# A hybrid decoder step on one core: the sample convolution gathered, tied ranks counted, masks fused, and the down projection built from 2x2 block products

## The chip, the cores and the metric

One core of one Trainium2 chip. The metric is the device time of one execution of the whole program in microseconds (us). Before the change it is 1780.9 us, the median of 3 runs (1780.2 to 1784.61).

## What is computed

One layer of a decoder serves a prompt of 1024 tokens and 8 sample sequences of one token each, with the same weights (model width 1024, all float32):

```
q, k, v, idx, gdn = split(rmsnorm(x) @ w_in)
o_attn = attention over the 256 best keys, chosen by the indexer's score
         (lax.top_k: among equal scores the lower position wins)
cq, ck, cv = silu(causal conv of width 4 over gdn's q, k, v)   # sample tokens: 3 stored columns + 1 new
o_gdn  = gated delta rule(cq, ck, cv)
x += concat(o_attn, o_gdn) @ w_out
x += cross attention into 256 memory tokens
x += (silu(rmsnorm(x) @ w_gate) * (rmsnorm(x) @ w_up)) @ w_down     # D_FF = 2816 = 22 * 128
```

A prompt token chooses 256 keys out of up to 1024, a sample token 256 out of 4097.

## The kernel before

Activations lie transposed, 128 features on the partitions and the 1032 tokens along the columns. A float32 product is made of three matmuls: weights and activations are each split into a high part (a cast on ScalarE, line 125 for weights, 143 for activations) and a low part (the difference, GpSimd in line 126 for weights, VectorE in line 144 for activations), and high x high, high x low and low x high are summed in PSUM. `load_w` fetches a weight tile on SyncE's queue (SP) and splits it; `wh` and `wl` have two buffers each.

The program is written as generators that take turns (`run`), with the two top-k searches as side threads. The Tile framework then orders the instructions of each engine by priority and by its own timeline; each engine runs its list in that order, each wait in its place.

**The front** (0 to about 518 us) projects all columns of w_in. `gdn_front` makes the convolution for each of 12 column tiles; in a tile's last group it also convolves the 8 sample tokens, with four VectorE operations of 8 columns (lines 734 to 737). `stage_topk` searches the 256th best score of each prompt row bit by bit and writes a mask (lines 397 to 423). `stage_sample_topk` does the same for the sample tokens in seven-way steps: `count` compares 257 columns with up to seven thresholds, one VectorE operation each (line 1267), sums across partitions by a matmul and takes a digit. It runs the search three times: over the high 16 bits, over the low 16 bits, and (`radix(y, 13)`, line 1313) over the positions of the scores that are equal to the last one taken, 1 + 4 x 7 counts in five rounds. Its last operation is line 1314. Then the pools of the front are released, and attention begins with `stack_k` (lines 497 to 500) and `stack_q` (line 509) in their place.

**Attention and the memory part** run to about 1190 us and aren't touched but for names of scratch tensors.

**The gated units** (`unit_product`, to about 1512 us): gate and up projections of 2 x 128 features in each of 11 units, by products of 2x2 blocks (Strassen's form in Winograd's version, 7 products for 8). A unit leaves three of its four result blocks (the first is made earlier, in `early`); GpSimd multiplies them (line 1900) and SP stores them to `scrF`, features by tokens.

**The down projection** (`stage_down`, `down`) is plain. It goes through the 22 feature tiles in three passes (8, 7 and 7), each over 8 output tiles; a pass loads a weight tile of 8 or 7 x 128 x 128, multiplies it in three column groups (512, 256, 264) and adds each bank to the residual `xT` (line 1913). `fetch` brings activations back from `scrF` and splits them. The last pass ends each output tile with `store_y`: nine transposes on TensorE, copies, and DMAs.

```
self.down(0, acts, (0,))        # 8 feature tiles, first 512 columns
self.down(0, acts, (1, 2))
self.down(8, more, (0, 1, 2))   # 7
self.down(15, acts[:7], (0, 1, 2), True)
```

Of the kernel before, what the change touches and what calls it, by code (L numbers as in the profile page):

```python
# [6 lines left out]
F32 = mybir.dt.float32  # L7
# [32 lines left out]
class Kernel:  # L40
# [112 lines left out]
    def consts(self):  # L153
        nc, c = self.nc, self.c
        jp = c.tile([128, 128], I32, name="jp")
# [175 lines left out]
    def stage_topk(self):  # L331
# [62 lines left out]
        for j, i in enumerate(tl):  # L394
            nk = (i + 1) * 128
            eq = self.tk.tile([128, 1024], BF, name="tkeq", tag="eq")
            V.tensor_scalar(eq[:, :nk], hi[i], H[:, j:j + 1], None, op0=OP.is_equal)
            w = self.tk.tile([128, 1024], U16, name="tkw", tag="w")
            V.tensor_scalar(w[:, :nk], lo[i], sg[:, j:j + 1], ag[:, j:j + 1], op0=OP.mult, op1=OP.add)
            V.tensor_mul(lo[i], w[:, :nk], eq[:, :nk])  # L400
            yield
# [4 lines left out]
        for j, i in enumerate(tl):  # L406
# [4 lines left out]
            x = self.tk.tile([128, 1024], BF, name="tkx", tag="x")[:, :nk]  # L411
            pj, hj = P[:, j:j + 1], H[:, j:j + 1]
            V.tensor_scalar(eq, hi[i], hj, None, op0=OP.is_equal)
            V.tensor_scalar(x, lo[i], pj, None, op0=OP.is_equal)
            V.tensor_mul(eq, eq, x)
# [3 lines left out]
            V.tensor_scalar(x, lo[i], pj, None, op0=OP.is_gt)  # L419
            V.tensor_add(m, m, x)  # L420
            V.tensor_scalar(x, hi[i], hj, None, op0=OP.is_gt)
            V.tensor_add(m, m, x)
# [281 lines left out]
    def gdn_front(self, h):  # L704
# [3 lines left out]
        for kind, col, ct in (("k", C_GK, 4 + h), ("q", C_GQ, h), ("v", C_GV, 8 + h), ("z", C_GZ, None)):  # L708
            wh, wl = self.load_w(w_in[:, col + 128 * h:col + 128 * h + 128], KD, 128)
            j = "kqvz".index(kind)  # L710
            for g, (g0, n) in enumerate(GROUPS):
# [7 lines left out]
                else:  # L719
# [11 lines left out]
                    if g == 2:  # L731
                        st = self.stT[:, ct].rearrange("p (b j) -> p j b", j=3)
                        ys, us = y[:, m:n], raw[:, 4 + m:4 + n]
                        V.tensor_scalar(ys, st[:, 0], w[0], None, op0=OP.mult)
                        V.scalar_tensor_tensor(ys, st[:, 1], w[1], ys, op0=OP.mult, op1=OP.add)
                        V.scalar_tensor_tensor(ys, st[:, 2], w[2], ys, op0=OP.mult, op1=OP.add)
                        V.scalar_tensor_tensor(ys, us, w[3], ys, op0=OP.mult, op1=OP.add)
                        nc.gpsimd.tensor_copy(self.ctail[:, :, ct], raw[:, 1 + m:4 + m])
                        nc.gpsimd.tensor_copy(self.cnew[:, :, ct], us)
                    self.silu(y[:, :n], y[:, :n])  # L740
                nc.scalar.dma_start(self.scrG[h, j, :, g0:g0 + m], y[:, :m])
                if g == 2:
                    nc.gpsimd.tensor_copy(self.gsam[:, h, j], y[:, m:n])
                yield

# [428 lines left out]
    def sample_consts(self):  # L1174
# [49 lines left out]
        y = iota("i_pos", [128, 8, 32], [[-2, 8], [-128, 32]], 8191, 0)  # L1224
# [4 lines left out]
        V.tensor_scalar(off[:, 0:1], u, -16.0, None, op0=OP.mult)  # L1229
        V.tensor_scalar(u, pr, 3, 1, op0=OP.logical_shift_right, op1=OP.bitwise_and)  # L1230
        V.tensor_sub(off[:, 0:1], off[:, 0:1], u)
        self.rpos = I([128, 260], F32, name="rpos")
        V.memset(self.rpos, 8191.0 - 4096.0)
        V.tensor_scalar(self.rpos[:, 0:256], y.rearrange("p a b -> p (a b)"), off[:, 0:1], None, op0=OP.add)
# [10 lines left out]
    def stage_sample_topk(self):  # L1245
# [12 lines left out]
        y = kp.tile([128, 260], U16, name="sk_y")  # L1258
# [542 lines left out]
    def first(self, u, kind, s1, p, sg):  # L1801
# [5 lines left out]
        else:  # L1807
            V.tensor_add(sg[:, 1], s1, p)  # L1808
            self.nc.gpsimd.tensor_mul(sg[:, 1], sg[:, 0], sg[:, 1])
            self.nc.sync.dma_start(self.scrF[2 * u, :, 0:HN], sg[:, 1])  # L1810

    def unit_product(self, u):
# [9 lines left out]
        for kind in ("gate", "up"):  # L1822
# [69 lines left out]
            c = [u1, u2[:, :HN], s1]  # L1892
            if kind == "gate":
                for x in c:
                    self.silu(x, x)
                sg["c"] = c
            else:
                f = 2 * u
                for x, y, dst in zip(c, sg["c"], (self.scrF[f, :, HN:], self.scrF[f + 1, :, 0:HN], self.scrF[f + 1, :, HN:])):
                    nc.gpsimd.tensor_mul(x, x, y)  # L1900
                    nc.sync.dma_start(dst, x)

    def down(self, f0, acts, groups, last=False):
        nc, V = self.nc, self.nc.vector
        kt = len(acts)
        for o in range(KD):
            wh, wl = self.load_w(self.i["w_down"][0][128 * f0:128 * (f0 + kt), 128 * o:128 * o + 128], kt, 128)
            for g in groups:
                g0, n = self.G[g]
                p = self.bank("g", "pd")  # L1910
                self.proj(wh, wl, 0, 128, g, p, kt=kt, act=lambda k: [x[:, g0:g0 + n] for x in acts[k]])
                x = self.xT[:, o, g0:g0 + n]
                V.tensor_add(x, x, p[:, :n])  # L1913
            if last:
                self.store_y(o)

    def store_y(self, o):
        nc = self.nc
        cs = slice(128 * o, 128 * o + 128)
        for half in range(2):  # L1920
            p = self.bank("g", "py")
            for t in range(4):
                c = 128 * (4 * half + t)
                self.tr(p[:, 128 * t:128 * t + 128], self.xT[:, o, c:c + 128], 128)
            y = self.unit("y", [128, 4, 128])
            (nc.vector.tensor_copy if half else nc.scalar.copy)(y, p.rearrange("p (t c) -> p t c", c=128))
            nc.sync.dma_start(self.o["y_prompt"][0, 512 * half:512 * half + 512, cs].rearrange("(t p) c -> p t c", p=128), y)
        p = self.bank("g", "py")
        self.tr(p[:NS, :128], self.xT[:, o, T:NT], 128)
        y = self.unit("y8", [NS, 128])  # L1930
        nc.scalar.copy(y, p[:NS, :128])
        nc.scalar.dma_start(self.o["y_sample"].rearrange("b o d -> (b o) d")[:, cs], y)

    def fetch(self, f, h, l, s):

        a = self.unit("af")[:, :s.stop - s.start]
        self.nc.sync.dma_start(a, self.scrF[f, :, s])
        self.split(a, h[:, s], l[:, s])

    def stage_down(self, after_units):  # L1940

        acts = [(self.AH[:, k], self.AL[:, k]) for k in range(KD)]
        n1, n2, n = slice(0, HN), slice(HN, NT), slice(0, NT)
        for f in range(8):
            self.fetch(f, *acts[f], n1)
        after_units()
        for o in range(KD):
            self.nc.sync.dma_start(self.xT[:, o, n1], self.scrT[:, o, n1])  # L1948
        for f in range(8):
            self.fetch(f, *acts[f], n2)  # L1950
        self.down(0, acts, (0,))
        for o in range(KD):
            self.nc.sync.dma_start(self.xT[:, o, n2], self.scrT[:, o, n2])
        self.down(0, acts, (1, 2))
        more = [[self.du.tile([128, UW], FR, name="d" + x, tag="d")[:, :NT] for x in "hl"] for _ in range(7)]
        for f in range(8, 15):
# [140 lines left out]
```

## Time and profile before

| | |
|---|---|
| median of 3 runs | 1780.9 us |
| the profiled execution | 1789.59 us, of which its span 1787.4 us |
| busy: PE, PEld, DVE, ACT, POOL | 91%, 81%, 62%, 49%, 46% of the span |
| matmuls | 11316 |
| granted TensorE clock, mean | 0.952 of full speed |
| DMA | 206.44 MB, mean 115 GB/s |

The profile is of one execution, 8.7 us above the median. PE is TensorE's matmuls, PEld its weight loads, which run beside them; DVE is VectorE, ACT ScalarE, POOL GpSimd. A share of the whole span is a mean over stages with different limits, so the stages are looked at one by one. Matmuls are pipelined: the duration of one is longer than its distance to the next, and it is the distance that counts.

### The profile page before, as it was taken

To read this page: it belongs to the slowest core of one execution; us is meant where nothing else is said; L and a number is where in the kernel's file an instruction comes from. 1 tells how busy PE (TensorE), PEld (TensorE's weight loads), DVE (VectorE), ACT (ScalarE), POOL (GpSimd) and SP (SyncE) were. 2 spreads that over 40 slices of the span, in tenths; PEclk is the share of its full clock that TensorE was granted. 3 is DMA by queue.
4 is the path that set the end of the run, shared out by engine and by line. 5 is a ranking of instruction groups with operands and counts; after the bars stand their busy time and mean duration, and the time that the engine had idled before them with its cause. 6 is when DMAs were issued, how large, how long until landed. Compare 5 with 4: busy or idle time off the path is not lost. (4 is left out here: it accounts for less than half of the span.)

```text
span 1787.4 us, 31531 instructions
## 1 busy us (share of the span) xinstructions
PE 1634.5 (91%) x11316; PEld 1442.3 (81%) x11316; DVE 1106.3 (62%) x2913; ACT 880.8 (49%) x2069; POOL 827.7 (46%) x791
## 2 busy tenths in 40 slices
PE   6999988768859999989998899879999999899998
PEld 5989877768747777768896578669999999599998
DVE  7699996999979777762355523775556666313111
ACT  5568879964546666664565564432222323212111
POOL 1277663573147133225553436765656566342210
PEclk9999998879979899979998999989999999999999
DMA  4134354324242324256322244553444444922132
GB/s 156 46 91 130 118 145 125 119 90 134 85 121 63 82 72 122 78 156 184 89 83 59 79 140 148 190 160 101 137 125 126 130 131 132 313 82 86 42 90 58
DMA packets 268630, 206.44 MB, mean 115 GB/s; under 512 B 31397, under 2 KB 240506, under 8 KB 268338
## 3 DMA queue, kind: packets, MB, share of 16 engines
q1 hardware_dynamic: 249674, 175.34, 32.6%
q0 software_dynamic: 4864, 14.69, 2.9%
q10 hardware_dynamic: 13936, 14.40, 2.3%
q8 instruction: 89, 1.46, 0.3%
q14 instruction: 67, 0.55, 0.1%
HBM read 152.01 MB, written 52.47 MB: 114 GB/s over the span
## 5 line engine op out<-in xcount | busy, mean ns | idle before, releaser
L126 POOL TENSOR_TENSOR wl<-raw,wh 128x1024 fp32r<-128x1024 f32 (+2 forms) x107 | 255.3, 2387 | 401.8 <-ACT wh L125 329.0
L48 PE MATMUL pm<-AH,wh 128*128 128x384 f32 (+7 forms) x792 | 269.8, 341 | 4.6 <-ACT y L111 4.0
L48 PE MATMUL pm<-AH,wl 128*128 128x384 f32 (+7 forms) x792 | 263.0, 332 | 0.1
L48 PE MATMUL pm<-AL,wh 128*128 128x384 f32 (+7 forms) x792 | 262.7, 332 | 0.1
L125 ACT CAST wh<-raw 128x1024 fp32r<-128x1024 f32 (+2 forms) x107 | 110.0, 1029 | 255.5 <-PE pd L48 172.4
L48 PEld LDWEIGHTS pm<-AH,wh 128*128 128x128 f32 (+1 forms) x792 | 154.0, 195 | 12.0 <-ACT y L111 4.6
L1842 POOL TENSOR_TENSOR sl<-S,sh 128x512 fp32r<-128x512 f32 x88 | 119.7, 1371 | 89.6 <-ACT sh L1841 86.9
L48 PEld LDWEIGHTS pm<-AL,wh 128*128 128x128 f32 (+1 forms) x792 | 154.0, 194 | 6.7 <-issue 0.8
L48 PEld LDWEIGHTS pm<-AH,wl 128*128 128x128 f32 (+1 forms) x792 | 152.9, 193 | 5.1 <-issue 0.7
L1913 DVE TENSOR_TENSOR xT<-xT,pd 128x256 f32<-128x256 f32 (+2 forms) x72 | 36.8, 512 | 190.5 <-PE pd L48 190.4
L1841 ACT CAST sh<-S 128x512 fp32r<-128x512 f32 x88 | 53.3, 619 | 183.5 <-DVE S L1836 170.6
L48 PE MATMUL pd<-AH,wh 128*128 128x512 f32 (+2 forms) x360 | 116.3, 325 | 5.1 <-ACT wh L125 5.1
L48 PE MATMUL pd<-AH,wl 128*128 128x512 f32 (+2 forms) x360 | 115.4, 322 | 3.7 <-POOL wl L126 3.7
L48 PE MATMUL pd<-AL,wh 128*128 128x512 f32 (+2 forms) x360 | 115.1, 321 | 0.0
L1836 DVE TENSOR_TENSOR S<-raw 128x512 f32<-128x512 f32 x44 | 54.8, 1246 | 92.0 <-DMA raw<-in_w_gate 38.0
L48 PE MATMUL p<-AL,sh 128*128 128x260 f32 x352 | 99.7, 283 | 0.0
L48 PE MATMUL p<-AH,sh 128*128 128x260 f32 x352 | 99.6, 283 | 0.0
L48 PE MATMUL p<-AH,sl 128*128 128x260 f32 x352 | 99.3, 283 | 0.0
L48 PE MATMUL pg<-AH,wh 128*128 128x512 f32 x176 | 73.3, 419 | 14.6 <-DVE sg L1808 7.5
L1866 DVE TENSOR_TENSOR uu<-uu,p 128x260 f32<-128x260 f32 x176 | 71.9, 420 | 16.4 <-PE p L48 14.7
L48 PEld LDWEIGHTS pd<-AH,wh 128*128 128x128 f32 x360 | 68.1, 189 | 11.9 <-ACT wh L125 6.8
L48 PEld LDWEIGHTS pd<-AH,wl 128*128 128x128 f32 x360 | 67.9, 189 | 10.6 <-POOL wl L126 5.3
(703 smaller groups left out, 5153.8 us busy)
## 6 DMA issues: line engine op xcount, KB each, us to landing
raw<-in_w_gate SPq DMA_DIRECT2D x33, 512.0 KB
raw<-in_w_up SPq DMA_DIRECT2D x33, 512.0 KB
raw<-in_w_in SPq DMA_DIRECT2D x24, 512.0 KB
raw<-in_w_out SPq DMA_DIRECT2D x16, 512.0 KB
raw<-in_w_down SPq DMA_DIRECT2D x16, 512.0 KB
af<-scrF SPq DMA_DIRECT2D x14, 516.0 KB
raw<-in_w_down SPq DMA_DIRECT2D x16, 448.0 KB
scrG<-y ACTq DMA_DIRECT2D x32, 192.0 KB
```

Source lines behind the costliest of these rows:

```text
L48: return self.nc.tensor.matmul(out, lhsT, rhs, start=start, stop=stop)
L125: self.nc.scalar.copy(wh, raw)
L126: self.nc.gpsimd.tensor_sub(wl, raw, f32(wh))
L1836: op(t, x, y)
L1841: nc.scalar.copy(h, x)
L1842: nc.gpsimd.tensor_sub(l, x, f32(h))
L1866: V.tensor_add(out[:, c], x[:, c], p[:, :w // 2])
L1913: V.tensor_add(x, x, p[:, :n])
```

## The change

Four edits. (1) The 48 small operations of the sample convolution become seven over all 12 tiles at once, and three SiLUs. (2) Ties of the sample top-k are ranked by a running sum along the columns and seven small matmuls across partitions, in place of the third search. (3) In the prompt's masks a comparison and the product or sum after it become one instruction. (4) The down projection is made of seven products of 2x2 blocks. The units now store seven operands of 11 x 128 features to `scrD` (one of 512 columns from `early`, one more of 512, five of 520), with one more subtraction on GpSimd and three operations on VectorE for each unit; the weights' sums are made on VectorE while the stage runs, in two half steps of 6 and 5 feature tiles for each of four output tiles; `fetches` bring the next product's operands while one is computed.

```
 gdn_front, last group of a tile:
-  V.tensor_scalar(ys, st[:, 0], w[0], None, op0=OP.mult)
-  V.scalar_tensor_tensor(ys, st[:, 1], w[1], ys, ...)
-  V.scalar_tensor_tensor(ys, st[:, 2], w[2], ys, ...)
-  V.scalar_tensor_tensor(ys, us, w[3], ys, ...)
+def conv_sample(self):            # once, before the last z tile
+  for t in range(4):
+    V.tensor_tensor(z if t else y, x[t], w, op=OP.mult)      # 128 x 12 x 8
+    if t:
+      V.tensor_add(y, y, z)
+  for j, c in enumerate((4, 0, 8)):
+    self.silu(self.gsam[:, :, j], y[:, c:c + 4])
 stage_topk, each of six tiles (three such pairs more, and one ahead of the second search):
-  V.tensor_scalar(x, w, need[:, j:j + 1], None, op0=OP.is_le)
-  V.tensor_mul(m, x, eq)
+  V.scalar_tensor_tensor(m, w, need[:, j:j + 1], eq, op0=OP.is_le, op1=OP.mult)
 stage_sample_topk:
-  V.tensor_mul(y[:, :N], eq[:, :N], self.rpos[:, :N])
-  yield from radix(y, 13)
-  V.scalar_tensor_tensor(sel[:, :N], y[:, :N], P, sel[:, :N], op0=OP.is_ge, op1=OP.add)
+  V.memset(run[:, 0:1], 0.0)
+  V.tensor_copy(ep.rearrange("p (g j) -> p j g", j=8), eq[:, :256]...)
+  V.tensor_tensor_scan(run[:, 1:], ones, ep, 0.0, op0=OP.mult, op1=OP.add)
+  ...                                        # 4 bf16 matmuls of 256 columns, 3 of 1
+  V.scalar_tensor_tensor(w[:, :256], p[:, :256], need, eq[:, :256], op0=OP.is_le, op1=OP.mult)
+  V.scalar_tensor_tensor(w[:, 256:257], ...)
+  V.tensor_add(sel[:, :N], sel[:, :N], w[:, :N])
+def down_blocks(self, u, b11, up, gate):      # end of each unit; store() is a DMA on SP
+  G.tensor_mul(b12, b12, t3); G.tensor_mul(b22, b22, t2); G.tensor_mul(b21, b21, t4)
+  store(5, b22); store(6, b21)
+  V.tensor_sub(t3, b22, b12); store(3, t3)
+  V.tensor_sub(b12, b12, b11); store(1, b12)
+  G.tensor_sub(t2, b22, b12); store(2, t2)
+  V.tensor_sub(t4, b21, t2); V.tensor_scalar(t4[:, HN:], t2[:, HN:], -1.0, ...); store(4, t4)
 stage_down:
+order = ((0, HN, "A11"), (4, w, "A22"), (1, w, "S1"), (2, w, "S2"), (5, w, "S4"), (3, w, "S3"), (6, HN, "A12"))   # w = 520
+def weights(name, m, ks):                     # S: SBUF, get(i, j): DMA of a block into one of 3 buffers
+  A11, A12: split of the block;  A22: DMA into t = S[:, m, ks]
+  S1: V.tensor_add(t, t, get(2, 1))    S2: V.tensor_sub(t, t, get(1, 1))
+  S4: V.tensor_sub(t, get(1, 2), t)    S3: V.tensor_sub(t, get(1, 1), get(2, 1))
+  return self.split_w(t)
+def finish(name, m, banks):                   # banks added to x (residual) or U, on VectorE
+  A11: ACT copy; S1: two adds a bank; A22, S2, S3: one G.tensor_add more; S3: one V.tensor_add more
+for q, (_, n, name) in enumerate(order):
+  for m in range(4):
+    for ks in (slice(0, 6), slice(6, 11)):
+      wh, wl = weights(name, m, ks)
+      for p, c in zip(banks, halves):         # 1 x 512 or 2 x 260 columns
+        for k in range(ks.start, ks.stop):
+          self.three(p, wh[k], wl[k], h[:, c], l[:, c], ...)
+      one residual DMA, two fetches of the next product
+      store()                                 # output halves that are done
+    done += finish(name, m, banks)
 build: du has 6 buffers (was 14), on the side of the released pools; xT, U, S and wd beside it
```

## Rows read from the trace of the kernel before

**Rows 1.** the page's span in 40 slices of 44.7 us, busy tenths
```profile
PE   6999988768859999989998899879999999899998
...
DVE  7699996999979777762355523775556666313111
```

**Rows 2.** view of stages: busy us of each engine (instructions), then PEclk, DMA share, GB/s
```profile
330.00:465.00 135.00, 101.17 (x579) 93.34 (x578) 130.83 (x449) 85.44 (x235) 62.56 (x89) 0.85 0.35 108
465.00:503.00 38.00, 32.62 (x182) 29.92 (x182) 31.97 (x128) 16.33 (x61) 5.39 (x12) 0.90 0.36 115
503.00:518.00 15.00, 0.00 (x0) 0.00 (x0) 9.96 (x25) 4.86 (x12) 12.10 (x23) 0.50 0.52 143
1200.00:1500.00 300.00, 298.96 (x2493) 298.63 (x2492) 179.24 (x342) 83.62 (x145) 180.35 (x134) 1.00 0.40 123
1512.00:1558.00 46.00, 37.24 (x157) 28.09 (x155) 21.12 (x26) 15.74 (x17) 16.80 (x9) 0.99 0.91 317
1558.00:1782.00 224.00, 224.00 (x1506) 205.94 (x1505) 47.23 (x80) 35.02 (x45) 55.67 (x26) 0.99 0.25 74
```

**Rows 3.** chain that ended last, in order of time: start us, us, what
```profile
1262.45 214.59 PE p L48 x1788
...
1716.98 9.89 PE pd L48 x63
1726.87 1.07 PE py L51 x9
```

**Rows 4.** groups by form, 1557 to 1705 us
```profile
L126 POOL TENSOR_TENSOR wl<-raw,wh 128x1024 fp32r<-128x1024 f32 x10 | 23.9, 2395 | 36.8 <-ACT wh L125 36.8
...
L126 POOL TENSOR_TENSOR wl<-raw,wh 128x896 fp32r<-128x896 f32 x10 | 21.4, 2136 | 69.0 <-ACT wh L125 69.0
...
L125 ACT CAST wh<-raw 128x896 fp32r<-128x896 f32 x11 | 10.4, 941 | 79.9 <-PE pd L48 79.9
...
L125 ACT CAST wh<-raw 128x1024 fp32r<-128x1024 f32 x9 | 9.5, 1052 | 40.3 <-PE pd L48 39.6 <-DMA raw<-in_w_down 0.6
```

**Rows 5.** timeline, VectorE, 1470 to 1512 us: start us, us, what
```profile
1474.29 0.69 DVE L1836 TENSOR_TENSOR S<-S,raw 128x512 f32<-128x512 f32 x1
...
1477.11 1.77 DVE L1836 TENSOR_TENSOR S<-raw 128x512 f32<-128x512 f32 x1 [0.52 <-POOL sl L1842]
...
1508.06 3.26 DVE L144 TENSOR_TENSOR AL<-af,AH 128x520 fp32r<-128x520 f32 x4 [6.14 <-ACT AH L143]
```

**Rows 6.** timeline, GpSimd, 1470 to 1512 us
```profile
1475.77 2.55 POOL L1842 TENSOR_TENSOR sl<-S,sh 128x512 fp32r<-128x512 f32 x2 [5.75 <-ACT sh L1841]
```

**Rows 7.** groups by form, 1200 to 1470 us
```profile
L1900 POOL TENSOR_TENSOR uu<-uu 128x520 f32<-128x520 f32 x9 | 11.8, 1309 | 0.0
```

**Rows 8.** groups by form, VectorE, 100 to 560 us
```profile
L1267 DVE TENSOR_SCALAR_CACHE_REDUCE sk_junk<-sk_y,sk_T 128x257 f32<-128x257 uint16 x29 | 12.3, 477 | 0.1
...
L735 DVE SCALAR_TENSOR_TENSOR y<-stT,vc,y 128x8 f32<-128x8 f32 x11 | 8.6, 786 | 0.0
...
L734 DVE TENSOR_SCALAR y<-stT,vc 128x8 f32<-128x8 f32 x11 | 4.9, 447 | 0.0
```

**Rows 9.** timeline, VectorE, 502 to 504 us
```profile
503.09 0.49 DVE L1314 SCALAR_TENSOR_TENSOR sk_sel<-sk_y,sk_P,sk_sel 128x257 f32<-128x257 uint16 x1
```

**Rows 10.** timeline, VectorE, 470 to 482 us
```profile
475.35 0.49 DVE L419 TENSOR_SCALAR tkx<-low,tk_P 128x1024 bf16<-128x1024 uint16 x1
...
475.89 0.68 DVE L420 TENSOR_TENSOR tkm<-tkm,tkx 128x1024 bf16<-128x1024 bf16 x1
```

**Rows 11.** line 730, a fused operation over two SBUF operands: min/median/max ns
```profile
L730 DVE SCALAR_TENSOR_TENSOR y<-raw,vc,y x72: 467/606/4203, 82.1 to 345.0; 128x384 f32<-128x384 f32 x48, 128x256 f32<-128x256 f32 x24
```

**Rows 12.** timeline, ScalarE, 499 to 517 us
```profile
499.54 0.49 ACT L431 ACTIVATE sq<-pm 128x384 f32<-128x384 f32 x1 [3.23 <-PE pm L48]
503.66 0.41 ACT L497 CAST kh<-kn 64x256 fp32r<-64x256 f32 x1 [3.63 <-DVE sk_sel L1314]
...
516.66 0.62 ACT L509 CAST qst<-qld 64x512 fp32r<-64x512 f32 x1 [9.33 <-DMA qld<-qscr]
```

More of the change, by code (lines that the diff above doesn't have):

```diff
@@ L154, in consts @@
         nc, c = self.nc, self.c
-        jp = c.tile([128, 128], I32, name="jp")
+        jp = self.unit("jp", [128, 128], I32)
         nc.gpsimd.iota(jp, pattern=[[1, 128]], base=0, channel_multiplier=-1)
@@ L708, in gdn_front @@
         for kind, col, ct in (("k", C_GK, 4 + h), ("q", C_GQ, h), ("v", C_GV, 8 + h), ("z", C_GZ, None)):
+            if h == 3 and ct is None:
+                self.conv_sample()
             wh, wl = self.load_w(w_in[:, col + 128 * h:col + 128 * h + 128], KD, 128)
@@ L1228, in sample_consts @@
         V.tensor_scalar(u, pr, 7, None, op0=OP.bitwise_and)
[L1229 to L1234, printed above, removed]
+        V.tensor_copy(off[:, 0:1], u)
+        self.rank = [I([128, 128], BF, name=f"rank{m}") for m in range(4)]
+        for m, op in zip(self.rank, (OP.is_lt, OP.is_gt, OP.is_equal)):
+            V.scalar_tensor_tensor(m, y, off[:, 0:1], self.blk16, op0=op, op1=OP.mult)
+        V.scalar_tensor_tensor(self.rank[3], self.upper, -1.0, self.rank[2], op0=OP.add, op1=OP.mult)
         self.iota16 = self.keep.tile([128, 16], F32, name="iota16")
@@ L1311, in stage_sample_topk @@
         V.scalar_tensor_tensor(sel[:, :N], hi[:, :N], H, sel[:, :N], op0=OP.is_gt, op1=OP.add)
-        V.tensor_mul(y[:, :N], eq[:, :N], self.rpos[:, :N])
-        yield from radix(y, 13)
-        V.scalar_tensor_tensor(sel[:, :N], y[:, :N], P, sel[:, :N], op0=OP.is_ge, op1=OP.add)
+        run = kp.tile([128, 257], BF, name="sk_run")
+        V.memset(run[:, 0:1], 0.0)
+        ep = kp.tile([128, 256], BF, name="sk_ep")
+        V.tensor_copy(ep.rearrange("p (g j) -> p j g", j=8), eq[:, :256].rearrange("p (j g) -> p j g", g=32))
+        V.tensor_tensor_scan(run[:, 1:], self.ones[:, 0:1].to_broadcast([128, 256]), ep, 0.0, op0=OP.mult, op1=OP.add)
+        p = self.bank("sk", "prk")
+        less, more, same, odd = self.rank
+        for m, x in ((less, run[:, None, 0:256:8].to_broadcast([128, 8, 32])), (more, run[:, None, 8:257:8].to_broadcast([128, 8, 32])),
+                     (same, run[:, 1:].rearrange("p (g j) -> p j g", j=8)), (odd, eq[:, :256].rearrange("p (j g) -> p j g", g=32))):
+            self.mm(p[:, 0:256].rearrange("p (j g) -> p j g", g=32), m, x, m is less, m is odd)
+        for m in (less, more, same):
+            self.mm(p[:, 256:257], m, run[:, 256:257], m is less, m is same)
+        V.scalar_tensor_tensor(w[:, :256], p[:, :256], need, eq[:, :256], op0=OP.is_le, op1=OP.mult)
+        V.scalar_tensor_tensor(w[:, 256:257], p[:, 256:257], need, eq[:, 256:257], op0=OP.is_lt, op1=OP.mult)
+        V.tensor_add(sel[:, :N], sel[:, :N], w[:, :N])
         yield
@@ L1903, in down @@
[L1903 to L1915, printed above, removed]
@@ L1918, in store_y @@
+    def store_y(self, o, half):
         nc = self.nc
         cs = slice(128 * o, 128 * o + 128)
-        for half in range(2):
-            p = self.bank("g", "py")
[L1922 to L1938, printed above, removed]
-    def stage_down(self, after_units):
[L1942 to L1945, printed above, removed]
-        after_units()
[L1947 to L1956, printed above, removed]
-            self.fetch(f, *more[f - 8], n)
-        self.down(8, more, (0, 1, 2))
-        for f in range(15, 22):
-            self.fetch(f, *acts[f - 15], n)
-        self.down(15, acts[:7], (0, 1, 2), True)
@@ new lines, in store_y @@
+        p = self.bank("g", "py")
+        for t in range(4):
+            c = 128 * (4 * half + t)
+            self.tr(p[:, 128 * t:128 * t + 128], self.xT[:, o, c:c + 128], 128)
+        y = self.unit("y", [128, 4, 128])
+        nc.scalar.copy(y, p.rearrange("p (t c) -> p t c", c=128))
+        nc.sync.dma_start(self.o["y_prompt"][0, 512 * half:512 * half + 512, cs].rearrange("(t p) c -> p t c", p=128), y)
+        if half:
+            p = self.bank("g", "py")
+            self.tr(p[:NS, :128], self.xT[:, o, T:NT], 128)
+            y = self.unit("y8", [NS, 128])
+            nc.scalar.copy(y, p[:NS, :128])
+            nc.scalar.dma_start(self.o["y_sample"].rearrange("b o d -> (b o) d")[:, cs], y)
```

168 lines of the change are left out of this document (134 added, 34 removed).

## The prediction

> **What bounds the kernel now.** I read the page's slices first, then the stages, the chain that ended last, and the rows of the stages that the change touches. The slices [rows 1] show two kinds of stage. From 313 to 491 us (slices 8 to 11) VectorE stands at 9 and PE at 6 to 8: VectorE sets the pace. From 1200 us to the end PE stands at 9, with one dip near 1550. The stages say it in numbers [rows 2]: VectorE is busy for 131 of 135 us from 330 to 465, with PE at 101 and a clock of 0.85; from 1200 to 1500 PE has 299 of 300; from 1558 to 1782 it has 224 of 224. Between lie two holes: no matmul from 503 to 518, and from 1512 to 1558 only 157. The chain [rows 3] is PE work in the last 500 us, so there its content is the time.
>
> **The sum's base.** The rows are of an execution of 1789.6 us with a span of 1787.4 (2.2 outside it), 8.7 above the median of 1780.9. I work out a difference and take it from the median; the 0.5% between the two is far below the bounds.
>
> **The down projection: content.** In the units, 1788 matmuls of 260 columns take 214.59 us, 0.120 apart. An output tile of the last pass is 7 x 3 triples of 512, 256 and 264 columns in 9.89 us, 0.471 a triple; less two short ones, a 512 stands 0.231 apart [rows 3]. Before: 22 x 8 x 3 = 528 triples, 248.7 us. After: two products with 512 columns, 2 x 4 x 11 x 3 = 264 x 0.231 = 61.0; five with 2 x 260, 5 x 4 x 11 x 3 x 2 = 1320 x 0.120 = 158.4; together 219.4. The count of matmuls, 1584, stays; half of the long ones become short. **-29**. The transposes of the output (1.07 a tile [rows 3]) stay, and so does the end: one output half's copy and DMA after the last sum.
>
> **The start of it.** From 1512 to 1558 the 157 matmuls are of 512 columns: 157 x 0.231 = 36.3 of 46 us, so 9.7 are lost, with the DMA engines at 0.91 and 317 GB/s [rows 2] bringing activations and residual at once. The new first product needs no residual and only three operands that couldn't come before the units' pools were free; the second product's, the last of which waits for unit 10's chain of seven operations and stores on SP, have 30 us of cover (264 / 2 x 0.231). Bounds 0 and 9.7 lost; I take 4, since three fetches with their splits are a fifth of what had to come before. **-6**.
>
> **Its stream.** Each half step now needs a new split in the time of the one before, with two buffers; before, a split had 9.9 us. From 1024 and 896 columns [rows 4] ScalarE's cast costs 0.87 ns a column more and GpSimd's difference 2.0: for 768 columns 0.83 + 1.88, with handoffs (estimate 0.3) 3.0 us, against 5 x 3 x 2 x 0.120 = 3.6 us of PE in a half step of five. That holds if GpSimd is free. But VectorE over two SBUF operands and GpSimd take turns: a sum of 512 columns took 0.69 alone and 1.77 [rows 5] when it met two GpSimd differences of 2.55 [rows 6]. So I add what excludes each other, for one output tile (PE 66 x 0.120 = 7.9): GpSimd's two differences 3.5, VectorE's splits of 11/4 operands at 0.815 (3.26 for four [rows 5]) 2.2, the weights' sums 1.9 (0.69 scaled from 512 to 1408 columns), one sum more on GpSimd 1.3 [rows 7]. A11 and A12: at most 5.7. A22: 7.0. S1 and S4: 7.6. S2: 8.9. S3, with one more on VectorE: 9.7. S2 is over by 1.0, S3 by 1.8, four tiles each: **+11**. The floor is 0, if these overlap better than in the one row; the ceiling stands with the rivals. DMA hides: the stream's share was 0.25 at 74 GB/s before [rows 2]; the operands and the doubled weights (77 operands of 0.26 MB, 32 weight blocks of 0.72 MB, 8.4 MB of residual and output) make some 52 MB in 235 us, 220 GB/s, under the 317 seen.
>
> **The units.** Each unit gets one GpSimd operation (1.3 [rows 7]) and three on VectorE of 520 columns (0.8 [rows 5]), and SP three stores and a load more. In the 300 us, 10.4 units of 28.8, GpSimd has 180 busy and VectorE 179 [rows 2]; they come to 194 and 204. PE's 299 covers that. What could come through is SP: a store that waits for the new chain stands ahead of the next unit's weights, which PE needs. Bounds 0 and 8 (0.7 a unit); **+2**.
>
> **The front: VectorE.** The third search goes: 29 counts, 12.3 us [rows 8], and two operations like the last one, 0.49 [rows 9]. In come six operations of at most 257 columns, at about 0.49: net 10, and with the five rounds' small operations I take 12 (10 to 15). The convolution's four lines cost 4.9 (line 734) to 8.6 (line 735) each [rows 8], 20 to 34 us, for 8 columns each, mostly waiting. Line 730 runs in the same tiles from 82 to 345 us [rows 11], so some five of the twelve lie after 223 us, 8 to 14, against about 2 for the new form (seven of 96 columns, by the 0.49 for 257). I take 8 there and nothing for the tiles before, where PE stands at 9 [rows 1]. The fused masks are even: the pair for 1024 columns is 0.49 + 0.68 = 1.17 [rows 10]; a fused operation took 0.49 for 257 columns [rows 9] and 0.606 for 384 [rows 11], 0.92 ns a column, so 1.20 for 1024. Taken: 0, bounds -5 (the pair meets the port twice) and +3.
>
> The Trainium skill's page "Vector Engine (DVE) Microarchitecture Reference", section "Points that are easy to get wrong", says that this fused form halves its throughput when both SBUF sources are other than bfloat16, and that speaks against the one fused product over two 16-bit integers. By it the 4224 columns of the six tiles would cost their 0.92 ns once more, 3.9 us of VectorE, and the sum would be 1744. Rows 11 don't bear it out: two float32 sources, and 384 columns still took 606 ns at the median.
>
> So 20 us of VectorE go, nearly all where it sets the pace and PE has room (101 of 135 busy [rows 2]). That room, 0.25 of the time, and PE's own chains take part of what VectorE frees; I turn 0.6 of it into time: **-12** (0 if PE's own chain decides, 20 at most).
>
> **The front: its end.** ScalarE has the last query tile's square at 500.03 and then stands until 503.66, because its next cast waits for the last operation of the sample's search [rows 9, 12]; attention's own first cast comes at 516.66, and PE is idle to 518 [rows 2]. Without the third search that wait is gone and the pools are free before PE's projections end; next is the last query tile's way through scratch (the 9.33 us [rows 12]), which stays. Bounds 3.6 and 9; **-5**.
>
> **Sum.** -29 - 6 + 11 + 2 - 12 - 5 = -39: 1742 us.
>
> **Rivals.** *The port takes the down projection's gain.* If GpSimd's and VectorE's turns cost an average of 0.6 us more in each of the 56 half steps than the packed sums allow, 34 us, the down projection ends 10 above before, and front and units leave -5: 1776; at half that price 1759. For: the slack is 0.6 us by the rows, and one GpSimd sum of 1.3 exceeds it. Against: the units run at 299 of 300 with GpSimd at 60% of the time, though with seven buffers for two.
>
> *The weights' sums are late (slower).* If a half step's sum isn't made ahead but stands in VectorE's list behind the finish of the last tile and two splits, the chain from PE's end is 1.6 (splits) + 1.0 + 0.83 + 1.88 + 0.3 = 5.6 plus two additions of 260 columns, by the nearest row 0.49 each [rows 9], 6.6 us against a mean 4.0. In S1, S2, S4 and S3 that is 32 half steps x 2.6 = 83: -29 - 6 + 83 + 2 - 17 = +33, 1814. It decides from 50/32 = 1.6 us a half step on. For: lists are fixed ahead by a timeline that may not know the port. Against: the sums go into a buffer as large as the whole weight half, so nothing but VectorE's place and the DMA keeps them from running far ahead.
>
> *The front gives nothing.* PE's projections run to 500 us in any case, and VectorE's freed time falls where PE's chains of norm and scratch decide: 1742 + 17 - 3 = 1756.
>
> **Chances.** Forecast 0.58 (1720 to 1755), the port 0.21 (1755 to 1785), the front 0.12, late sums 0.09. A measurement of this kernel can tell about 0.3%, 5.3 us, from no change. Faster: 0.58 + 0.12 + 0.15 of the port's = 0.85; the same 0.07 (the rest of the port's and 0.01 of the late sums); slower 0.08. The range reaches from the forecast without the overrun and with the front at its best (-39 - 11 - 12 = -62: 1719) to the port's case at its full price, 1776; what is left out is the late sums and the port's worst, under 0.2 together.
>
> **What would show it.** Right: 1584 matmuls of the down projection at 0.120 and 0.231; PE gaps in its stream that end on GpSimd's `wl`, in S2 and S3 above all; first query cast of attention near 500 and not 516; PE still at 299 of 300 in the units. Wrong: gaps in S1 to S3 that end on VectorE's sums or on `raw` DMAs; units in which PE waits for `sl`; an attention that begins no earlier.

## The result, and the profile after

The changed kernel takes 1800.7 us (median of 4 runs, 1799.0 to 1803.1) against 1780.6 before: ratio 1.0096 [1.0077, 1.0116], slower by 17.1 us [13.7, 20.7] by the ratio and by 20.1 by the medians. The forecast was 1742 us, with a range from 1719 to 1776 and a chance of 0.08 for slower. It was wrong, and in sign.

The profiled execution lasted 1799.8 us (span 1798.1). The page's slices of the changed kernel, to be read against [rows 1]:

```profile
PE   6999989787779999989998899798999987899898
...
DVE  7788987999788777822356234956666677557540
PEclk9999998799989999979999999899999999999999
```

From slice 26 on, where PE stood at 9 with one dip, there are now several slices of 7 and 8. The stages, against [rows 2] (us, then busy us of PE, PEld, DVE, ACT, POOL with their instructions, then PEclk, DMA share, GB/s):

```profile
330.00:465.00 135.00, 104.38 (x598) 94.14 (x597) 133.56 (x439) 88.58 (x265) 56.97 (x85) 0.87 0.37 115
...
486.00:501.00 15.00, 1.73 (x5) 0.80 (x4) 10.79 (x26) 5.35 (x13) 14.08 (x27) 0.65 0.52 139
...
1170.00:1537.00 367.00, 332.08 (x2639) 329.21 (x2640) 240.33 (x398) 89.51 (x155) 215.82 (x155) 0.96 0.45 139
1537.00:1580.00 43.00, 35.58 (x137) 26.61 (x137) 19.42 (x25) 16.00 (x25) 19.55 (x13) 0.92 1.08 337
1580.00:1677.00 97.00, 95.63 (x793) 95.07 (x792) 65.40 (x87) 37.75 (x59) 50.05 (x28) 1.00 0.67 200
1677.00:1724.00 47.00, 38.86 (x280) 37.30 (x280) 21.34 (x26) 12.53 (x22) 16.38 (x10) 0.89 0.56 162
1724.00:1792.00 68.00, 68.00 (x451) 61.82 (x449) 17.54 (x25) 23.80 (x41) 32.96 (x19) 1.00 0.39 110
```

The third row holds the units. PE was busy there for 299 of 300 us before; now it stands for 35 of 367. The fourth and the sixth row are the first and the fifth product of the down projection, the only two of seven in which PE stands long.

The stages of every run, from the first matmul of each stage to the first of the next (to the end of its last in the down projection). "Attention begins" is its first matmul, from the span's start. Times are medians of the timed runs, ratios are against runs of the kernel before on the same chip; e3 and e9 have a single run each. The stages are of the one profiled execution. One run of e11 is left out, a slow one of 2204.65 us.

| run | time, us | ratio to before | attention begins | units | down |
|---|---|---|---|---|---|
| before | 1780.6 | | 518 | 322.3 | 268.9 |
| e9, before again | 1787.3 | | 515 | 322.1 | 269.2 |
| changed | 1800.7 | 1.0096 [1.0077, 1.0116] | 500 | 367.3 | 255.1 |
| e1 | 1768.7 | 0.9945 [0.9929, 0.9962] | 501 | 320.8 | 269.0 |
| e4 | 1781.5 | 1.0009 [0.9994, 1.0025] | 507 | 321.7 | 269.7 |
| e8 | 1770.9 | 0.9944 [0.9928, 0.9960] | 508 | 321.1 | 269.2 |
| e2 | 1775.8 | 0.9979 [0.9958, 1.0000] | 500 | 345.5 | 249.3 |
| e3 | 1760.3 | | 499 | 322.9 | 256.4 |
| e5 | 1796.2 | 1.0087 [1.0061, 1.0114] | 498 | 360.1 | 258.3 |
| e6 | 1787.2 | 1.0036 [1.0020, 1.0051] | 499 | 347.5 | 260.9 |
| e7 | 1792.1 | 1.0060 [1.0040, 1.0079] | 500 | 364.7 | 247.9 |
| e10 | 1789.4 | 1.0040 [1.0017, 1.0062] | 497 | 356.4 | 255.0 |
| e11 | 1777.1 | 0.9973 [0.9956, 0.9989] | 500 | 355.5 | 244.0 |
| e12 | 1780.3 | 0.9985 [0.9961, 1.0009] | 500 | 353.7 | 244.7 |
| e13 | 1766.5 | 0.9912 [0.9894, 0.9931] | 501 | 337.7 | 249.5 |
| e14 | 1764.5 | 0.9898 [0.9879, 0.9916] | 498 | 332.1 | 253.9 |
| e15 | 1789.4 | 1.0046 [1.0026, 1.0066] | 499 | 358.7 | 251.0 |

So the units lost 45 us, the down projection gained 14, and the front gained. PE's waits for the adds that empty its banks, in the units (in sum, times, longest), first of e9, then of the changed kernel:

```profile
PE p L48 <- DVE uu L1866: 1.0, 1, 1.0
```

```profile
PE p L48 <- DVE uu L1881: 34.1, 12, 5.4
```

Where the units stand is seen in one unit. VectorE's timeline of the changed kernel:

```profile
1341.69 0.41 DVE L1881 TENSOR_TENSOR uu<-s,p 128x260 f32<-128x260 f32 x1
1342.03 1.45 DVE L1927 TENSOR_TENSOR uu<-s,uu 128x520 f32<-128x520 f32 x1
1343.41 0.41 DVE L1881 TENSOR_TENSOR uu<-s,p 128x260 f32<-128x260 f32 x1
1343.74 1.44 DVE L1929 TENSOR_TENSOR uu<-uu,b 128x512 f32<-128x512 f32 x1
1346.66 1.73 DVE L1933 TENSOR_TENSOR uu<-uu,s 128x512 f32<-128x512 f32 x1 [1.48 <-POOL s L1931]
1348.32 1.22 DVE L1934 TENSOR_SCALAR uu<-s 128x8 f32<-128x8 f32 x1
1349.46 0.87 DVE L1881 TENSOR_TENSOR uu<-uu,p 128x260 f32<-128x260 f32 x2
```

L1927 to L1934 are VectorE's four operations of `down_blocks`: three subtractions and the sign change of the last eight columns (the section on the change speaks of three). They stand in VectorE's list between the next gate's first adds and its others. From 1343.8 to 1349.5 no bank is emptied, and PE, whose eight banks are all in use, stops.

GpSimd's timeline shows why the four take so long. The first line is GpSimd at the same moment; the second is VectorE's sign change in the last unit, when GpSimd does nothing:

```profile
1347.81 1.71 POOL L1857 TENSOR_TENSOR sl<-S,sh 128x512 fp32r<-128x512 f32 x1
```

```profile
1545.53 0.16 DVE L1934 TENSOR_SCALAR uu<-s 128x8 f32<-128x8 f32 x1
```

The sign change begins while GpSimd makes a low part of the weights (L1857) and ends 0.03 us after it, at 1349.54; so it is in each of the first ten units (1.22 to 1.23 us), and alone it takes 0.16. L1927 and L1929 take 1.45 and 1.44 us beside GpSimd and 0.70 and 0.69 in the last unit without it. The adds from a bank (L1881) take 0.42 us with GpSimd at work or not. So most of the four operations' time is waiting for GpSimd: by the last unit's rows they would take some 2.2 us a unit alone (estimate, with L1933 like L1929), and they take 6.0.

The stretches around the stop:

```profile
1342.00:1346.00 4.00, 4.00 (x36) 4.00 (x35) 3.18 (x4) 1.53 (x3) 3.31 (x3) 1.00 0.63 198
1346.00:1350.00 4.00, 0.59 (x5) 0.39 (x5) 3.30 (x4) 0.00 (x0) 3.52 (x3) 1.00 0.60 199
1350.00:1354.00 4.00, 3.98 (x20) 4.00 (x21) 2.09 (x6) 0.64 (x1) 0.00 (x0) 0.57 0.79 234
```

PE is busy for 0.6 of the 4 us, and after the stop it runs 20 matmuls in 4 us instead of 36, at a granted clock of 0.57. Both parts are in the sums of the units: PE's idle time grew from 2.8 us (322.0 less 319.2, e9 below) to 34.9 (367.0 less 332.1), and its busy time by 12.9.

### The profile page after: what moved, and what is told of

Its sections match the earlier page's. It is cut to its first block, busy times and chain, and to the rows that moved or that the text cites. A ratio compares the mean times of both kernels' runs of the same rounds, so it can differ in the third digit from the quotient of the medians.

```text
span 1798.1 us, 31943 instructions
## 1 busy us (share of the span) xinstructions
PE 1613.5 (90%) x11313; PEld 1430.4 (80%) x11313; DVE 1185.9 (66%) x2866; ACT 920.1 (51%) x2155; POOL 892.5 (50%) x827
## 5 line engine op out<-in xcount | busy, mean ns | idle before, releaser
L126 POOL TENSOR_TENSOR wl<-raw,wh 128x1024 fp32r<-128x1024 f32 (+2 forms) x91 | 209.4, 2302 | 247.7 <-ACT wh L125 244.1
L1857 POOL TENSOR_TENSOR sl<-S,sh 128x512 fp32r<-128x512 f32 x88 | 126.4, 1446 | 97.3 <-ACT sh L1856 89.4
L125 ACT CAST wh<-raw 128x1024 fp32r<-128x1024 f32 (+2 forms) x91 | 90.7, 997 | 105.4 <-PE pd L48 22.7
L48 PE MATMUL pd<-AH,wh 128*128 128x260 f32 (+1 forms) x384 | 116.8, 308 | 6.9 <-ACT wh L125 6.9
L48 PE MATMUL pd<-AH,wl 128*128 128x260 f32 (+1 forms) x384 | 116.1, 311 | 6.3 <-POOL wl L126 6.2
L126 POOL TENSOR_TENSOR wl<-Sd,wh 128x768 fp32r<-128x768 f32 (+1 forms) x40 | 74.0, 1853 | 84.8 <-ACT wh L125 84.8
L48 PE MATMUL pd<-AL,wh 128*128 128x260 f32 (+1 forms) x384 | 115.7, 305 | 0.0
L48 PE MATMUL p<-T2h,sh 128*128 128x260 f32 x176 | 56.0, 318 | 33.9 <-DVE uu L1881 31.7
L48 PEld LDWEIGHTS pd<-AH,wh 128*128 128x128 f32 x384 | 73.7, 192 | 11.5 <-ACT wh L125 9.0
L48 PEld LDWEIGHTS pd<-AH,wl 128*128 128x128 f32 x384 | 72.4, 192 | 11.7 <-POOL wl L126 8.8
```

What stands on the lines that cost most here:

```text
L48: return self.nc.tensor.matmul(out, lhsT, rhs, start=start, stop=stop)
L125: self.nc.scalar.copy(wh, raw)
L126: self.nc.gpsimd.tensor_sub(wl, raw, f32(wh))
L1857: nc.gpsimd.tensor_sub(l, x, f32(h))
```

## The experiments

**The front and the units told apart.** e1 puts the three front edits alone into the kernel before; e4 has of these the ties alone, e8 the convolution alone; e9 is before, profiled once more. The diff against before is for e1 the change without `down_blocks` and the new `stage_down`, and for e4 and e8:

```
e4 + run, ep, scan, seven matmuls, rank tables;  - radix(y, 13)
e8 + conv_sample(), called ahead of z in the last head;  - lines 732 to 737
```

> The kernel before with the three edits ahead of the feed forward units alone (ties by a running sum, one sample convolution, fused masks); units and down projection as before. Theory 1 (front right as forecast, the loss lies wholly in the units): the first attention matmul comes 17 to 21 us earlier than before, as in the changed kernel, the units take 322 to 325 us again, and the time is about 1780.5 - 18 = 1762 us (1757 to 1767). Rival (the front's gain is lost in the units because they merely start earlier and run into the same limit): units of 335 us or more and a time within 4 us of before.

> The kernel before with the ties ranked by a running sum alone (the 13 step search for the tie's place is gone, the prefix by a scan and seven matmuls comes in). By the prediction's terms: 12 us less of VectorE on the path that ends the front, at the weight of 0.6 that the prediction took, and up to 5 us of the front's end: 7 to 12 us faster, 1769 to 1774 us. Rival (the front's gain comes from the sample convolution, which took its place on VectorE in all four heads): within 3 us of before.

> The kernel before with the sample tokens' convolution done once for all tiles alone. By the prediction's terms: 8 us less of VectorE at the weight of 0.6, about 5 us faster, 1774 to 1777. After the ties alone moved nothing in the median of many runs and the three front edits together moved 11.6 us: if the rest of that gain is here, 8 to 12 us faster, 1768 to 1773. Rival (it needs the ties' edit too, since either alone only moves the end of the front to the other chain): within 3 us of before.

> The kernel before, unchanged, in a second profiled execution. The one that the prediction read lasted 1789.6 us, 8.7 above its median. If these 8.7 us lay in its front, the first attention matmul comes near 520 us here in place of 528.8, the units take 321 to 323 us and the down projection 269 again, as in every other run with the old stages; then the front's edits are worth 9 to 11 us in the trace, as in the medians, and not 17.7. Rival (the 8.7 us lay spread over all stages): units or down projection shorter by 3 us or more.

e1 is 9.8 us faster by its ratio [6.8, 12.6], less than its theory's 13 to 23 (1757 to 1767), and its units take 320.8: an early start costs them nothing. The ties give nothing: slower by 1.6 us [-1.1, 4.5], where 7 to 12 us faster were expected. The convolution gives 10.0 [7.1, 12.8], all that the three give together. e9 half explains the traces: this execution too is above its median, attention begins 3.7 us earlier than in the one that the prediction read (525.1 for 528.8 in the trace's own count, 515 and 518 in the table), not 8.7, and units and down projection are the same within 0.3 us. What differs between executions of the kernel before lies in its front, so the 18 us between two traces there are partly chance; the medians say 10.

**The place of the differences.** e2 moves VectorE's four operations to GpSimd, e3 leaves the differences out, e6 makes them wait for the next gate's last p5 add:

```
e2  - V.tensor_sub(t3, b22, b12)           + G.tensor_sub(t3, b22, b12)      (L1929, L1933, L1934 alike)
e6  + V.tensor_scalar(zero, s1[:, w-1:w], 0.0, None, op0=OP.mult)            (next gate, after plus(s1, u2, p5))
    + V.scalar_tensor_tensor(t3, b22, zero, b12, op0=OP.add, op1=OP.subtract)
```

> The changed kernel with the four VectorE operations that form the block differences of the down projection moved to GpSimd, the stores as they are. Theory 1 (these four stand in VectorE's list ahead of the adds that empty the next gate's banks, wait there for GpSimd's data and for the shared port, and so stop TensorE with all banks full): the stops of 3 to 4 us in each unit go, the units take 322 to 332 us in place of 367, the time is about 1758 to 1768 us. Rival (the load of the new work itself, on whichever of the two engines that share the port, sets the units' pace): units of 355 us or more and a time of 1790 us or more.

> The changed kernel without the four differences of the up blocks and gate (one on GpSimd, three on VectorE) and without the sign change of the last eight columns: these operations are left out, all seven blocks are still stored and fetched at the same places. Theory 1 (the differences' place on VectorE): units of 320 to 326 us, time about 1755 to 1762 us. Rival (SP: a store that waits for the new chain holds back the next weights, or the traffic of the six stores per unit): units stay at 350 us or more, because the stores are the same.

> The changed kernel with VectorE's four operations of down_blocks made to come after the next gate's adds of p5 and p7, by an operand (zero, one column) that is made from the last of these adds. Same engines, same number of operations and one column more. Theory 1 (it is the place in the list, ahead of the adds that empty the banks): units of 320 to 332 us, time 1755 to 1768 us. Rival (the load on VectorE and the port): units of 350 us or more wherever the four stand, time 1783 or more. Rival 3 (SP: the stores now come still later, and the next weights stand behind them): units of 340 us or more with VectorE waiting over 100 us in all for gate and up weights.

e3: units of 322.9 us with all six stores in place. The whole 44 us come with these five operations, not with the traffic or the stores as such. But e2 and e6 give back only half (345.5 and 347.5): each falls between its theory (332 at most) and its rival (355 or 350 at least). The place is part of it, and something else holds the units when the place is mended. In e6 VectorE still has 222.8 us of work in the units, and PE waits for it 22 times, 20.4 us; of its rival 3 the units (340 or more) came, but not the wait for weights (86.0 us and not over 100). In e2 VectorE's work is that of before, but it waits 68.9 us for the gate's weights, 37.9 before (e9), and SP's queue shows what stands ahead of them (its timeline, stretches of the queue's own DMA issues):

```profile
1305.32 0.38 SPq L1841 DMA_DIRECT2D raw<-in_w_gate  x1
1307.76 2.82 SPq L1921 DMA_DIRECT2D scrD<-uu  x2
1310.63 0.42 SPq L1912 DMA_DIRECT2D b<-scrD  x1
1311.51 0.38 SPq L1841 DMA_DIRECT2D raw<-in_w_gate  x1
```

The two halves of the gate's weights are issued 6.2 us apart, with two stores and the fetch of b11 between them that wait for GpSimd. VectorE's sums need both halves:

```profile
1316.37 0.69 DVE L1851 TENSOR_TENSOR S<-raw 128x512 f32<-128x512 f32 x1 [7.47 <-DMA raw<-in_w_gate]
```

**VectorE's list as the measure.** What the list holds in the units can be added up. The kernel before (e9), first the waits of VectorE (in sum, times, longest), then the stretch of the units:

```profile
DVE S L1836 <- DMA raw<-in_w_gate: 37.9, 10, 5.3
DVE S L1836 <- DMA raw<-in_w_up: 31.5, 8, 6.1
DVE uu L1866 <- PE p L48: 22.4, 25, 3.8
DVE S L1836 <- POOL sl L1842: 21.7, 19, 2.4
DVE AL L144 <- ACT AH L143: 16.0, 5, 6.2
```

```profile
1188.40:1510.40 322.00, 319.23 (x2638) 318.85 (x2639) 187.73 (x356) 90.17 (x157) 194.28 (x143) 0.99 0.41 127
```

187.7 of work and 129.5 of these waits are 317 of 322 us. Of the 134 us in which VectorE is "not busy" only the 22.4 in which it waits for matmuls are spare by this count, 2.0 us a unit. In the changed kernel first the same waits, then the four operations as groups by form (count, busy us, mean ns, idle time before):

```profile
DVE S L1851 <- DMA raw<-in_w_up: 43.6, 11, 4.6
DVE S L1851 <- DMA raw<-in_w_gate: 26.3, 10, 3.5
DVE S L1851 <- POOL sl L1857: 23.0, 19, 2.4
DVE uu L1933 <- POOL s L1931: 13.1, 9, 1.5
DVE uu L1881 <- PE p L48: 10.0, 9, 3.9
```

```profile
L1933 DVE TENSOR_TENSOR uu<-uu,s 128x512 f32<-128x512 f32 x10 | 18.0, 1799 | 13.1 <-POOL s L1931 13.1
...
L1927 DVE TENSOR_TENSOR uu<-s,uu 128x520 f32<-128x520 f32 x10 | 15.2, 1521 | 0.0
...
L1929 DVE TENSOR_TENSOR uu<-uu,b 128x512 f32<-128x512 f32 x10 | 14.4, 1441 | 0.0
L1934 DVE TENSOR_SCALAR uu<-s 128x8 f32<-128x8 f32 x10 | 12.3, 1225 | 0.0
```

18.0 + 15.2 + 14.4 + 12.3 + 13.1 = 73 us in ten units, 7.3 a unit, where 2.0 were spare. The count is rough: it would make the loss 5.3 a unit, 58 in eleven, and it was 45. The waits for weights came to the same in sum (69.9 and 69.4 us), those for matmuls fell by 12.4 and those for ScalarE's casts by 9.0 (16.0 to 7.0). e5 takes the wait out (t4 from b21 - b11 and t3, the sign change from t3), e10 moves L1934 to ScalarE, e15 has both and the fetches of e7:

```
e5   + G.tensor_sub(t4[:, :HN], b21[:, :HN], b11)
     - V.tensor_sub(t4, b21, t2)            + V.tensor_sub(t4, t4, t3)
e10  - V.tensor_scalar(t4[:, HN:], ...)     + nc.scalar.mul(t4[:, HN:], t2[:, HN:], -1.0)
```

> The changed kernel with the block for A22 formed in another way: GpSimd first takes b21 - b11, VectorE then takes its own t3 from that and negates t3's last eight columns, so that none of its four operations in down_blocks waits any more for GpSimd's t2 in the middle of the list. Number of VectorE operations and their place in its list stay, GpSimd has one more. Theory 1a (the wait for GpSimd's difference, 13.1 us in sum in the changed kernel's list of VectorE's waits, with the bank adds behind it): the units lose that and about as much of half clock after each stop, 367 -> 340 to 350 us, time 1774 to 1785. Rival 1b (the length of the four operations themselves, 6 us a unit at the place where the next gate's banks fill): units stay at 358 us or more, time 1790 or more.

> The changed kernel with the sign change of eight columns (1224 ns each on VectorE in the changed kernel, 11 times) made by ScalarE. Theory 4 (VectorE's list, its work and the waits that stand in it, fills the whole unit, so that each us more in the list is about one us a unit): units 11 x 1.2 = 13 us shorter, 367 -> 352 to 357 us. Rival (these 1.2 us lie in a time in which VectorE would wait for the matmuls anyway): units of 363 us or more.

> The changed kernel with the differences kept on VectorE at their place, but without the wait in the middle (as in the fifth experiment, 7 us of units), the sign change on ScalarE (as in the tenth, 11 us) and the fetches of the seventh (7 us of the down projection). Theory 4 (VectorE's list fills the unit, so the gains add): units of 346 to 352 us, down projection 248 to 252, time 1771 to 1780 us. Rival (the two edits take away the same idle time): units of 355 us or more, time 1783 or more.

e10 is the plainest: an operation on eight columns is worth 10.9 us, 367.3 to 356.4, as the list's theory said (352 to 357); 1.06 of its 1.22 us were waiting for GpSimd. e5 misses: it gains 7.2 us, not 17 to 27, and lies on its rival's side, that of the operations' length (358 or more). Its operations, in ten units (groups by form):

```profile
L1928 DVE TENSOR_TENSOR uu<-s,uu 128x520 f32<-128x520 f32 x10 | 17.7, 1774 | 4.8 <-POOL uu L1922 4.8
L1930 DVE TENSOR_TENSOR uu<-uu 128x512 f32<-128x512 f32 x10 | 17.3, 1734 | 0.3
L1933 DVE TENSOR_TENSOR uu<-uu,b 128x512 f32<-128x512 f32 x10 | 6.8, 679 | 0.0
L1931 DVE TENSOR_SCALAR uu<-uu 128x8 f32<-128x8 f32 x10 | 3.4, 343 | 0.0
```

With the waits ahead of them these take 50 us instead of 73, but VectorE then waits 40.7 us for the gate's weights, 14.4 more than in the changed kernel. And e15 (358.7, expected 346 to 352, with the rival's 355 or more on its side) shows that the two gains don't add. The list's length isn't the whole measure: list and weights' loads bound each other.

**The queues around GpSimd's differences.** e11 has the differences on GpSimd, the four late stores on ScalarE's queue and the fetches of e7; e12 all six stores there. e13 and e14 are e11 and e12 with b11 in buffers of its own:

```
e11  - nc.sync.dma_start(self.scrD[j, ...])     + (nc.sync if j in (5, 6) else nc.scalar).dma_start(...)
e13  - b11 = self.unit("b11", [128, HN])        + b11 = self.gv.tile([128, HN], F32, tag="b11", bufs=2)
     - sh, sl: bufs=7                           + bufs=6
```

> The changed kernel with the four differences on GpSimd (as in the second experiment), the stores of these four issued by ScalarE's queue in place of SP's, and four fetches per half product in the fifth product (as in the seventh). Theory 3 (what was left of the loss when the differences stood on GpSimd, 345.5 against 322 us, is SP: two stores and the fetch of b11 wait between the two halves of the gate's weights, issued at 1315.7 and 1321.9): units of 320 to 330 us, down projection about 243, time 1744 to 1755 us. Rival (GpSimd's own list: 23.2 us of work in a unit delays the low parts of the weights): units of 340 us or more, time 1762 or more.

> As the run before, with all six stores of a unit on ScalarE's queue. Theory 3: units of 320 to 330 us, time 1744 to 1755 us. Rival (ScalarE, in whose list the stores stand between the casts of the next weights, waits there for GpSimd's products and holds the casts back): units of 335 us or more and waits of TensorE for ScalarE's sh over 10 us.

> The kernel of the eleventh experiment with b11 in two buffers of its own in place of the pool that it shares with the pair, whose release it waited for in SP's queue (paid for with six in place of seven buffers for the split weights). Theory 3 (SP: the fetch of b11 stood between the two halves of the gate's weights and waited 37.7 us in nine units): VectorE's wait for the gate's weights falls from 81 to 30 to 45 us, units of 320 to 332 us, time 1740 to 1755 us. Rival (GpSimd's list, 23 us of work in a unit and the splits of the weights behind it): units of 345 us or more, time 1765 or more.

> As the run before, with all six stores on ScalarE's queue, so that SP has nothing but loads in the units. Theory 3: as e13 or up to 5 us less, units of 318 to 330 us. Rival (ScalarE now holds the casts back, as it waits in its list for GpSimd): units longer than in e13 by 5 us or more.

(The two issue times in the first of these are in the trace's own count, 10.4 us more than in the timeline above.) e11 and e12 miss: 355.5 and 353.7, longer than e2 and on the side of their rivals (340 and 335 or more), though in e12 PE waits 2.9 us for `sh` and not over 10. With the stores gone other entries of SP's queue take their place, here in e11 (in sum, times, longest):

```profile
SPq L1886 <- DMA scrD<-s: 45.6, 8, 7.1
...
SPq L1912 <- POOL uu L1929: 37.7, 9, 4.5
```

Both load into the one pool of five buffers, and wait for a release: the pair until a store from its buffer has landed, b11 until GpSimd has read an earlier b11. With own buffers for b11 the units fall to 337.7 and 332.1, 18 and 22 us less, and in e13 SP's waits fall with them (the pair's from 45.6 to 5.5, b11's from 37.7 to 16.5), so the shared pool did hold the units. VectorE's wait for the gate's weights fell only from 81.3 to 64.1, not to 30 to 45, and the down projection gives back 5.5 and 9.2 us (249.5 for 244.0, 253.9 for 244.7), for a reason not looked into. e14's 332.1, with no store of a unit left on SP, is 5.6 below e13, against the rival that ScalarE would hold the casts back. Neither reaches its forecast (332, 330 at most). In e14 GpSimd has 246 us of work in 332, and VectorE still waits 61.1 us for the gate's weights (37.9 before). Whether the last 10 us are GpSimd's load or the six buffers wasn't told apart.

e14 is the best version of the study: 1764.5 us, 0.9898 [0.9879, 0.9916] of the kernel before, and by the quotient of the two ratios 0.980 of the changed kernel.

**The fifth product.** In the down projection the matmuls' distances are those of the forecast, an output tile of 512 columns in 7.62 us (33 x 0.231) and one of 2 x 260 in 7.91 (66 x 0.120) where nothing disturbs it. Of the 35.7 us beyond 219.4, 12.0 lie in the first product and 15.4 in the fifth. ScalarE's timeline of the changed kernel, third tile of the fifth:

```profile
1701.61 0.62 ACT L143 CAST AH<-af 128x520 fp32r<-128x520 f32 x1 [9.22 <-DMA af<-scrD]
1702.14 0.72 ACT L125 CAST wh<-Sd 128x640 fp32r<-128x640 f32 x1
```

The weights' cast, which PE needs, stands behind the cast of an operand of the next product whose DMA is late; that DMA stands in SP's queue behind weight loads for the sixth product, which wait for one of three buffers.

```
e7  - for g in (more[1], more[0], more[0])    + for g in (more[1],) + (more[0],) * (4 if q == 4 else 2)
```

> The changed kernel with four operand fetches in each half product of the fifth product (A12 - S2) in place of two, so that most of them stand in SP's queue ahead of the weight loads for the sixth, which wait for buffers. Theory 2 (the 13.5 us that the third and fourth tile of this product take over their matmuls are ScalarE's casts of late operands with the running product's weight cast behind them): the fifth product loses 8 to 12 of its 15.4 us of excess, time 1788 to 1793 us. Rival (the product is bound by the weights' own differences on VectorE or by the transposes and stores of the output): the excess stays above 12 us, time 1797 to 1803.

The fifth product's stretch in e7:

```profile
1677.80:1717.70 39.90, 34.83 (x281) 33.32 (x280) 18.68 (x24) 12.23 (x21) 17.03 (x10) 1.00 0.59 173
```

47.0 us become 39.9 and the clock is 1.00 instead of 0.89: 7.1 of the 15.4 us, a little under the 8 to 12 expected, and 1792.1 in all, inside 1788 to 1793. The other 8 us are spread over the four tiles.

## Why the prediction was wrong, step by step

- **The units, +2 (bounds 0 and 8): the step that failed.** Measured +45. Its sentence was "they come to 194 and 204. PE's 299 covers that." Work was forecast at 18.7 us a unit for GpSimd and 19.6 for VectorE (194 and 204 over 10.4 units) and came to 19.6 and 21.8 (216 and 240 over 11). Low, but above all the wrong measure: VectorE's list also holds its waits for weights, in order, and with them only 2.0 us a unit were spare (e9). The operations were priced at 0.8 us, by a row with little disturbance, though [rows 5] had 1.77 beside it; they took 1.2 to 1.8. The turns with GpSimd, which the prediction worked out for the down projection, it left out here. And it counted three operations: the fourth, the sign change, had no price, and e10 puts 10.9 us on it. "SP: a store that waits for the new chain" was seen as a risk of 8 us. In the changed kernel it held nothing that shows: VectorE's waits for weights are 69.9 us, 69.4 before. Once the differences are on GpSimd, SP's queue holds them for 18 to 22 us by a load that waits for its buffer (e13, e14) and for 5.6 by two stores (e14 against e13).
- **The rival that came nearest** was that of the late sums (1814): its mechanism, VectorE's list holding other work ahead of what PE needs, was put into the down projection's weights. There it did not come (the first two sums lose 1.2 and 0.6 us in all); it came one stage earlier.
- **Content of the down projection, -29: right.** 219.4 us by the distances above.
- **Its start, -6: wrong.** The first product loses 12.0 us against 9.7 before, so +2. The step was "needs no residual": its stretch moves 337 GB/s at a DMA share of 1.08, and beside the second product's operands and weights 16 pieces of the residual come in it (4.1 MB). That this traffic is the cause wasn't tested.
- **Its stream, +11: the size right, the place wrong.** Beyond content and start there are 23.7 us against 10.6 before (269.0 - 248.7 - 9.7), +13. But the second and third sum (S2, S3), where the turns with GpSimd (the port) were to cost 1.0 and 1.8 a tile, lose 0.6 and 3.5 us in all, the latter with the output's transposes: the turns of VectorE and GpSimd overlapped with the matmuls. It is the fifth product, by SP's order for 7.1 of its 15.4 us (e7). The size was luck.
- **The front, -12 and -5: -10 measured.** Its end is right: PE's hole ahead of attention is 12.7 us in place of 17.1, and the first query cast comes at 499.0 in place of 516.7. Either edit alone mends it (12.7 in e8, 13.1 in e4). The convolution's part came out in size: e8's 10.0 less the hole's 4.4 leave 5.6, and 8 x 0.6 = 4.8 were taken. The term that failed is the ties' 12 x 0.6 = 7: e4 gives nothing, though its hole is 4.0 us shorter and VectorE has 13 us less work from 60 to 520 us (400.7 against e9's 413.7), and e1 gives no more than e8. Why 12 us less of VectorE came to nothing stays open. The fused masks, taken as even, were tried only within e1, which with them and the ties is no faster than e8. Two 16-bit integer sources cost no more than one with a bfloat16 (both in the changed kernel):

```profile
L411 DVE SCALAR_TENSOR_TENSOR tkeq<-low,tk_P,tkeq 128x1024 bf16<-128x1024 uint16 x1 | 1.3, 1275 | 0.0
...
L398 DVE SCALAR_TENSOR_TENSOR low<-score,tk_H,tkw 128x1024 uint16<-128x1024 int16 x1 | 1.3, 1272 | 0.0
```

The rule weighed there, of the Trainium skill's page "Vector Engine (DVE) Microarchitecture Reference", section "Points that are easy to get wrong", is not borne out by these two rows.

The sum as measured is -29 + 2 + 13 + 45 - 10 = +21, against 20.1 between the medians and 17.1 [13.7, 20.7] by the ratio.

## What to carry to other kernels

An engine that is busy for 60% of a stage may have no room at all: add up its work and the waits that stand in its list in order, and count as spare, at first, only the time in which it waits for the engine that sets the pace. Price a new operation by the row of a like one at the moment where it will stand: here eight columns took 1.22 us beside GpSimd and 0.16 alone. Work added at the end of a loop's round comes to stand in the next round's list, ahead of what empties the banks there; ask of each queue, SP's among them, what stands behind the new entry. After a stage is mended, look for the next entry of the same queue that waits (here store, then fetch of b11), and settle small front gains by medians, since two executions of the same kernel differed there by 4 us.

## What the runs showed of the hardware

A VectorE operation on eight float32 columns in SBUF took 0.16 us with GpSimd idle; begun while a GpSimd subtraction ran, it ended 0.03 us after that one, whatever was left of it (0.93 to 1.23 us, in the changed kernel and e5). A subtraction of two SBUF operands of 512 columns took 0.69 us alone and 1.44 to 1.8 beside GpSimd, an add of 260 columns from a PSUM bank 0.42 either way. After a stop of PE of some 3.5 us the granted clock was 0.57 over the next 4 us, most of it thus at the level of 1.2 GHz; in the units as a whole 32 us of added standing cost 45.
